# An encoder of two attention layers with experts: half of the output projection moved into the last attention steps, and layer 1's attention walked by key head in a fixed TensorE order

## The chip, the cores and the metric

The kernel runs on one core of a Trainium2 chip. The core's engines work from queues of their own, each in order: TensorE (PE; its weight loads are listed as PEld), VectorE (DVE), ScalarE (ACT), GpSimd (POOL) and SyncE (SP, which issues most DMAs). They wait for each other by semaphores. The metric is the time of one execution on the device in microseconds.

## The reference

Two layers over 512 tokens of width 1024, in float32, with 16 heads of 64. Each layer is a token mixer and a mixture of experts, both with a residual and a layer norm, scaled and shifted by a vector that comes from `c` (adaLN).

```python
for i in range(DEPTH):
    mod = c_act @ ada_w[i] + ada_b[i]
    sh1, sc1, g1, sh2, sc2, g2 = jnp.split(mod[:, None, :], 6, axis=-1)
    h = x * (1 + sc1) + sh1
    y = neighbourhood_mixer(...) if i == 0 else gqa_mixer(...)      # both end in  o @ w_o
    x = layer_norm(ALPHA * x + (1 + g1) * y, ln_g[i, 0], ln_b[i, 0])
    h = x * (1 + sc2) + sh2
    y = hierarchical_moe(h, ...)       # 4 groups of 8 experts: best group, best two experts
    x = layer_norm(ALPHA * x + (1 + g2) * y, ln_g[i, 1], ln_b[i, 1])
```

The neighbourhood mixer of layer 0 attends in a window of 8 rows by 16 columns with a bias. The mixer of layer 1 has 16 query heads over 4 key heads (4 queries share a key), with RMS-normed and rotated queries and keys, and attends to all 512 tokens.

## The kernel before

Tokens lie in four tiles `X[t]` of 128 rows. Most products are made in three terms of split operands, high and low halves (`hTH`/`hTL`, `wh`/`wl`, `oH`/`oL`): high by high, high by low, low by high. So one out-projection is 4 tiles x 2 column halves `h` x 8 blocks `k` x 3 terms = 192 matmuls of 512 columns, written to `pw` (`pj` in the changed kernel). ScalarE copies the high half, VectorE or GpSimd subtracts it for the low one.

**Layer 0.** `mixer0` first makes the values, then `neighbours` walks 32 steps n, head pair i = n // 4 and column block b = n % 4. `flow` writes TensorE's order, and with it VectorE's, by hand: the scores of step n + 1, then part of the filler, `turn(n)` (the transposes of the exponentials `pr`), adaLN work, more filler, and `weigh(n)` (the product with the values, in `po`). The filler is `STREAM`, the projections of the later heads, dealt out at `RATE` matmuls to a step. `close(i)` divides a head pair by its sum. The adaLN vectors `mod` are made of 24 column blocks j: `ADAV` lists those that VectorE makes by multiply-adds (`adav`), `ADAP` the pairs that TensorE makes (`adap`, one pair at the end of a step). `router_weights` folds the norm into the router's weights. Behind the steps come a `flush`, the two rows of `g1`, and then per tile t the out-projection `sums(t, h)`, the update of `X`, `turnX` (transposes of X), `logits`, and `router`, whose mask `Mb` VectorE makes in some 25 small operations and TensorE then sums. The order on TensorE is by hand there too.

**Experts.** Token rows are gathered by a matmul (`gc`), then the first and second expert matmuls (`gu`, `pd`) run. The 192 weight tiles of 1 MB of a layer come over SP's queue, in the order of a list (`W`): a transfer starts when the buffer that is next in that list comes free. Buffers are the five of `w0` and those of pools that are free in that phase: `wy` (`NWY` of them), `qs`, `wh`, `ot`. A pool that is opened where another was waits for the last reader of that other.

**Layer 1.** `mixer1` projects keys, values and the four query blocks, each of 4 query heads, in full before the attention; `attention(t)` then takes query tile t over all 16 heads. Within the layer the compiler's scheduler sets TensorE's order; no order is written by hand. The out-projection of tile t - 1 and its router are free to run beside the attention of tile t. `split_z` makes the gather's operands `zH` (ScalarE) and `zL` (GpSimd) as soon as a tile is normed.

## Time and profile before

| what | us |
|---|---|
| time, median of 3 runs | 1670.57 (1665.85 to 1672.82) |
| the profiled execution | 1673.29 |
| its span, first to last instruction | 1671.6 |
| TensorE, VectorE, ScalarE, GpSimd busy | 1574.7, 700.6, 437.6, 162.3 |
| mean granted clock of TensorE | 0.972 |
| layer 0: first out-projection matmul, first expert matmul | 296.06, 376.75 |
| layer 1: first record, first score, first expert matmul | 867.85, 981.59, 1164.38 |

A row of the timeline gives a start, a length, the engine, the line, the operation as out<-in, how many records it holds and, in brackets, the wait before it with the operation that ended it. Matmuls overlap, so the cost of one is the distance from its start to the next start, not its length. A matmul of plain float32 operands leaves two records. The granted clock is 1.00 at 2.4 GHz and 0.50 at 1.2 GHz; over a window it is a mean of the two.

### The profile page before, as it was taken

What the parts mean: (1) busy time and instruction counts of PE and PEld (TensorE: products, weight loads), DVE (VectorE), ACT (ScalarE), POOL (GpSimd) and SP (SyncE); (2) the same over time, 40 slices, a digit from 0 to 9 for tenths busy, and PEclk for the clock granted to TensorE, in tenths of its full rate; (3) what the DMA queues carried; (4) which work ended last, traced back from release to release, by engine and by line L of the source; (5) the groups of instructions that cost most, each with busy time, mean ns of one, the idle gap of its engine ahead of it and who ended that gap; (6) DMA issues with size and microseconds to landing.
All of it is one profiled execution on the core that took longest, in us unless ns stands there. A gap on an engine that the chain in (4) does not pass through costs nothing. (4 is left out here: it accounts for less than half of the span.)

```text
span 1671.6 us, 21362 instructions
## 1 busy us (share of the span) xinstructions
PE 1574.7 (94%) x8490; PEld 906.6 (54%) x8490; DVE 700.6 (42%) x1605; ACT 437.6 (26%) x934; POOL 162.3 (10%) x99
## 2 busy tenths in 40 slices
PE   7899997989999999999979989998999999999995
PEld 4676664773544545455448866766354545545442
DVE  3434545574232322323256865666432232323235
ACT  2343335231110111111134475453011111101112
POOL 2322212010000000000014250011000000000001
PEclk9999997999999999999989989999999999999997
DMA  9587872357999999999932000035899999999981
GB/s 328 196 309 269 331 306 104 137 202 295 417 419 420 419 419 420 419 419 420 420 125 102 26 1 25 1 125 206 368 416 420 420 420 420 419 420 420 419 332 51
DMA packets 76198, 493.17 MB, mean 295 GB/s; under 512 B 9876, under 2 KB 11284, under 8 KB 18876
## 3 DMA queue, kind: packets, MB, share of 16 engines
q1 hardware_dynamic: 71916, 485.05, 71.4%
q10 hardware_dynamic: 4176, 6.69, 1.2%
q8 instruction: 69, 1.13, 0.3%
q14 instruction: 37, 0.30, 0.1%
HBM read 489.61 MB, written 2.10 MB: 294 GB/s over the span
## 5 line engine op out<-in xcount | busy, mean ns | idle before, releaser
L300 PE MATMUL gu<-w,xT 128*64 128x512 f32 x2048 | 445.0, 592 | 0.0
L300 PEld LDWEIGHTS gu<-w,xT 128*64 128x64 f32 x2048 | 146.8, 137 | 291.6 <-issue 287.0
L300 PE MATMUL pd<-w,hx 128*64 128x512 f32 x1024 | 228.0, 598 | 0.0
L1391 DVE TENSOR_TENSOR h<-h,gu 128x512 f32<-128x512 f32 x32 | 22.0, 688 | 370.4 <-PE gu L300 370.4
L300 PEld LDWEIGHTS pd<-w,hx 128*64 128x64 f32 x1024 | 70.9, 137 | 140.3 <-issue 136.7
L300 PE MATMUL gc<-OH,zH 128*128 128x256 f32 x480 | 121.5, 291 | 2.6 <-DVE OH L1276 2.6
L300 PE MATMUL gc<-OH,zL 128*128 128x256 f32 x480 | 118.6, 284 | 0.0
L300 PE MATMUL gc<-YH,OT 128*128 128x512 f32 x244 | 104.2, 427 | 1.0 <-DVE X L1358 1.0
L1358 DVE TENSOR_TENSOR X<-X,gc 128x512 f32<-128x512 f32 x128 | 87.4, 688 | 39.3 <-PE gc L300 39.3
L300 PEld LDWEIGHTS gc<-OH,zH 128*128 128x128 f32 x480 | 92.5, 193 | 14.9 <-issue 11.4
L300 PE MATMUL gc<-YL,OT 128*128 128x512 f32 x244 | 96.3, 394 | 0.0
L300 PEld LDWEIGHTS gc<-OH,zL 128*128 128x128 f32 x480 | 92.6, 193 | 0.0
L300 PE MATMUL pw<-w,oH 128*128 128x512 f32 x256 | 86.3, 408 | 0.0
L1414 ACT ACTIVATE YH<-h 128x512 fp32r<-128x512 f32 x32 | 20.2, 630 | 233.6 <-DVE h L1413 233.6
L300 PE MATMUL pj<-wh,hTH 128*128 128x256 f32 (+1 forms) x272 | 71.2, 304 | 9.1 <-ACT hTH L419 4.0
L1294 ACT ACTIVATE xT<-gc,A 128x256 f32<-128x256 f32 x60 | 33.8, 566 | 173.9 <-PE gc L300 173.9
L300 PE MATMUL pj<-wl,hTH 128*128 128x256 f32 (+1 forms) x272 | 68.0, 292 | 0.0
L300 PE MATMUL pj<-wh,hTL 128*128 128x256 f32 (+1 forms) x272 | 65.6, 293 | 0.8 <-DVE hTL L427 0.8
L300 PEld LDWEIGHTS gc<-YH,OT 128*128 128x128 f32 x244 | 45.8, 188 | 37.3 <-DVE X L1358 15.8
L1292 DVE TENSOR_SCALAR xT<-gc,A 128x256 f32<-128x256 f32 x60 | 32.5, 545 | 76.9 <-ACT xT L1294 76.5
L1390 ACT ACTIVATE h<-gu 128x512 f32<-128x512 f32 x32 | 19.1, 597 | 173.0 <-PE gu L300 173.0
L303 PE MATMUL pt<-c_ident,pr 128*128 128x128 f32 x384 | 59.5, 283 | 2.1 <-ACT pr L862 2.0
(345 smaller groups left out, 2355.9 us busy)
## 6 DMA issues: line engine op xcount, KB each, us to landing
w<-in_gu SPq DMA_DIRECT2D x256, 1024.0 KB, 14.3
w<-in_dn SPq DMA_DIRECT2D x128, 1024.0 KB, 13.5
w<-in_ada SPq DMA_DIRECT2D x40, 1024.0 KB, 7.9
wq<-in_wqk SPq DMA_DIRECT2D x16, 512.0 KB, 3.6
w<-in_wo SPq DMA_DIRECT2D x8, 1024.0 KB, 5.8
w<-in_adaq SPq DMA_DIRECT2D x6, 1024.0 KB, 12.0
bias<-in_nab ACTq DMA_DIRECT2D x24, 256.0 KB, 3.4
w<-in_wq SPq DMA_DIRECT2D x4, 1024.0 KB, 4.9
```

Source lines behind the costliest of these rows:

```text
L300: return self.nc.tensor.matmul(out, l, r, start=start, stop=stop, **kw)
L303: self.nc.tensor.transpose(out, in_, self.ident)
L1292: nc.vector.tensor_scalar(xT[q][:, k, :], ps, s, b, op0=OP.mult, op1=OP.add)
L1294: nc.scalar.activation(xT[q][:, k, :], ps, AF.Identity, scale=s, bias=b)
L1358: nc.vector.tensor_tensor(X[t][:, c], X[t][:, c], ps, op=OP.add)
L1390: nc.scalar.activation(h, gu[0], AF.Silu)
L1391: nc.vector.tensor_tensor(h, h, gu[1], op=OP.mult)
L1414: nc.scalar.activation(YH[j][:, c], y, AF.Copy)
```

## The change

In layer 0 the weights of the output projection are split from step 26 on (`late`, `beside`). Steps 26 and 27 get no filler, and steps 28 to 31 get 24 matmuls each of the out-projection over the first half of its inputs, heads 0 to 7 (kh = 0), as filler. The second half (kh = 1) follows the attention, with logits and routers between. X is updated once for each half. Two more adaLN blocks go to VectorE, now three operations a step until step 23, and `router_weights` makes both of its sums on VectorE and in one matmul of 72 columns.

In layer 1 keys and values are projected together, query blocks 0 and 1 before the attention and 2 and 3 within it. The attention goes by key head c: 64 steps n = 16c + 4t + j, scores two steps ahead, TensorE in an order written by hand. Eight matmuls of a projection fill each of steps 3 to 14 of c = 0 and 1; five of the out-projection fill each step from 36 on, 140 of 192. X times the gain, plus the bias, is made beside it, on GpSimd for tiles 1 to 3. All four routers come behind the attention. `NWY` of layer 1 goes from one to three, `qs` from four to two, and in the weight list `wy` now stands first. The first gates are made before the first expert matmul instead of behind it.

```diff
-NWY = (3, 1)
+NWY = (3, 3)
...
-ADAV = [(0, 6), (0, 7), (0, 8), (0, 9), (1, 0), (1, 1), (1, 2)]
-ADAP = {4: [(0, 4), (0, 5)], 8: [(0, 10), (0, 11)], 12: [(1, 4), (1, 5)], 15: [(1, 6), (1, 7)], 19: [(1, 8), (1, 9)],
-        23: [(1, 10), (1, 11)], 26: [(1, 3)]}
...
+ADAP = {4: [(0, 4), (0, 5)], 8: [(0, 10), (0, 11)], 12: [(1, 5), (1, 6)], 15: [(1, 7), (1, 8)], 18: [(1, 9), (1, 10)], 21: [(1, 11)]}
...
-RATE = (18, 15)
+RATE = (18, 17, 24)
...
-            rate = RATE[n >= 12]
+            if n == 26:
+                need(STREAM[-1])
+                it = late()
+            rate = 0 if 26 <= n < 28 else RATE[(n >= 12) + (n >= 28)]
             fill(rate // 2)
             if b == 0 and i:
                 close(i - 1)
...
-                    adav(ADAV[i], b // 2, 2 * (b % 2) + k)
+            for k in range(3 * n, min(3 * n + 3, 8 * len(ADAV))):
+                adav(ADAV[k // 8], k % 8 // 4, k % 4)
             aside(n)
             fill(rate - rate // 2)
             if n in ADAP:
...
+        return it
...
         self.fold_cols(A2[:, 0], A2[:, 1], self.lnc[:, l, 0], self.lnc[:, l, 1], self.col[l][:, 2], self.col[l][:, 3])
-        ps = pp.tile([P, 36], F32, name="pt")
-        for k in range(KD):
-            self.mm(ps, bcast(A2[:, 1, k:k + 1], [P, P]), wr[:, k, :], k == 0, k == KD - 1)
-        nc.vector.tensor_tensor(rb, ps, self.rb[l], op=OP.add)
+        wb = pool.tile([P, S], F32, name=("dacc", "hf")[l], bufs=3 - l)[:, 0:KD * 36].rearrange("p (k n) -> p k n", k=KD)
+        sm = pool.tile([P, 2, 36], F32, name="wrs")
+        nc.vector.tensor_tensor(wb, wr, bcast(A2[:, 1, :, None], [P, KD, 36]), op=OP.mult)
         nc.vector.tensor_tensor(wr, wr, bcast(A2[:, 0, :, None], [P, KD, 36]), op=OP.mult)
-        ps = pp.tile([P, 36], F32, name="pt")
-        for k in range(KD):
-            self.mm(ps, bcast(self.Zo[:, 32:33], [P, P]), wr[:, k, :], k == 0, k == KD - 1)
-        nc.scalar.activation(cs, ps, AF.Copy)
+        for n, z in enumerate((wr, wb)):
+            nc.vector.tensor_reduce(sm[:, n, :], z.rearrange("p k n -> p n k"), axis=AX.X, op=OP.add)
+        ps = pp.tile([P, 2, 36], F32, name="pt")
+        self.mm(ps, bcast(self.Zo[:, 32:33], [P, P]), sm, True, True)
+        nc.vector.tensor_tensor(rb, ps[:, 1, :], self.rb[l], op=OP.add)
+        nc.scalar.activation(cs, ps[:, 0, :], AF.Copy)
 
     def fold_cols(self, out_s, out_b, g, b, sc, sh):
...
         def aside(n):
-            i, b = n // 4, n % 4
-            if b == 1 and i and i % 2 == 0:
-                self.accs, self.accl = [(j, accs.pop((l, j))) for l, j in ADAV[i - 2:i]], ADAV[i - 1][0]
+            while flushed[0] < len(ADAV) and 8 * min(flushed[0] + 2, len(ADAV)) <= 3 * n:
+                i = flushed[0]
+                self.accs, self.accl = [(j, accs.pop((l, j))) for l, j in ADAV[i:i + 2]], ADAV[i][0]
...
-            if n == 26:
-                self.router_weights(0, pp)
-            if n >= 28:
-                step()
-
-        self.flow(split, chunk, scores, turn, weigh, close, adav, adap, aside, done)
+            if n == 25:
+                self.router_weights(0, pp, pool)
+            beside(n)
+
+        flushed = [0]
+        it = self.flow(split, chunk, scores, turn, weigh, close, adav, adap, aside, late)
...
+        def project(c):
...
+                for k in range(KD):
+                    b = slice(256 * (k % 4), 256 * (k % 4) + 256)
...
+                    wh, wl = hl[c][1 + k // 4]
+                    for h, x in ((hH, wh), (hH, wl), (hL, wh)):
+                        self.mm(po, h[:, k, 128 * t:128 * t + 128], x[:, b], k == 0 and h is hH and x is wh, k == KD - 1 and h is hL)
+                        if h is hL and t == NT - 1 and k % 4 == 3 and c != 1:
+                            ahead(max(2, c + 1), k // 4)
+                        if k < KD - 1 or h is hH:
+                            yield
+                qq[c].append(rope(ps, t, 0, ss[c]))
+                yield
+
+        def keys(t):
...
+        def weigh(u):
+            c = u // 4
+            po[u] = pp.tile([P, 2, P], F32, name="po", bufs=1)
+            for kt in range(NT):
+                for y in range(2):
+                    self.mm(po[u][64 * y:64 * y + 64], V[:, kt, 64 * c:64 * c + 64], PT[u][:, kt, 2 * y:2 * y + 2, :],
+                            kt == 0, kt == 3)
...
+            queries(0, t)
+        scores(0)
+        scores(1)
+        for n in range(64):
+            c, i = n // 16, n % 16
+            if i == 0:
+                if c < 2:
+                    it = project(c + 2)
+                elif c == 2:
+                    hqs.close()
+                    step = late()
+                    it = halves()
+                else:
+                    self.free.append(nq)
+            if n == 24:
+                self.router_weights(1, pp, pool)
+            if 32 <= n < 36:
+                step(2)
+            elif 36 <= n < 44:
+                step(1)
+            k = (0 if i < 3 else 8) if c < 2 else 0 if n < 36 else 5
+            if n + 2 < 64:
+                scores(n + 2)
+            run(it, k - k // 2)
+            turn(n)
+            if c < 3 and 2 <= i < 6:
+                queries(c + 1, i - 2)
+                if c == 2 and i == 5:
+                    rps.close()
+            run(it, k // 2)
+            if n % 4 == 1 and n > 4:
+                finish(n // 4 - 1)
+        self.free.append(nq)
+        return it, lambda: finish(15)
 
     def scaled(self, pool, pp, dst, po, rz):
...
+                pw = pp.tile([P, F], F32, name="pj")
+                ks = range(KD) if kh is None else range(4 * kh, 4 * kh + 4)
+                for k in ks:
+                    oH, oL = (z[:, k % 2, :] for z in o[k // 2, t]) if l else (z[:, k % 4, :] for z in o[k // 4, t])
...
+                    for n, (a, b) in enumerate(((oH, wh), (oH, wl), (oL, wh))):
+                        self.mm(pw, a, b, k == ks[0] and n == 0, k == ks[-1] and n == 2)
+                        if k < ks[-1] or n < 2:
+                            yield
...
+                y = self.mod[0] if l else wk.tile([P, F], F32, name="y")
+                if l and kh == 0:
+                    eng = nc.gpsimd if t else nc.vector
+                    eng.tensor_tensor(x, x, gb[:, 0, c], op=OP.mult)
+                    eng.tensor_tensor(x, x, gb[:, 1, c], op=OP.add)
                 nc.vector.tensor_tensor(y, pw, g1[:, c], op=OP.mult)
-                nc.vector.scalar_tensor_tensor(x, x, ALPHA, y, op0=OP.mult, op1=OP.add)
+                if l or kh:
+                    nc.vector.tensor_tensor(x, x, y, op=OP.add)
+                else:
+                    nc.vector.scalar_tensor_tensor(x, x, ALPHA, y, op0=OP.mult, op1=OP.add)
+                yield
...
+            def halves():
+                for kh in range(2):
+                    for t in range(NT):
+                        for h in range(2):
+                            yield from sums(t, h, kh)
...
+            def late():
...
+                w, step = self.split_wo(l, whp)
+                lg, g1 = gain1()
+                if l:
+                    gb = wk.tile([P, 2, D], F32, name="gb")
+                    for n in range(2):
+                        for h in range(2):
+                            ps = pp.tile([P, F], F32, name="pj")
+                            self.row(ps, 0, 16 + 2 * n + h)
+                            nc.scalar.activation(gb[:, n, 512 * h:512 * h + 512], ps, AF.Copy, scale=ALPHA)
+                    return step
+                return halves()
...
+            def beside(n):
+                if n == 26 or n == 27:
+                    step(4)
+                    for t in range(2 * n - 52, 2 * n - 50):
+                        ready(0, t)
+                elif n > 27:
+                    step(2)
...
+                with tc.manual_schedule(engines={mybir.EngineType.PE}):
+                    it, finish = self.mixer1(st, qs, nq, pp, o, late, halves)
+                    hx = turnX(0)
+                    run(4)
+                    logits(0, lg[:, 0, :], hx)
+                    finish()
+                    for t in range(2, NT):
+                        run(6)
+                        hx = turnX(t - 1)
+                        run(8)
+                        logits(t - 1, lg[:, t - 1, :], hx)
+                        run(4)
+                        self.router(t - 2, wk, pp, "pt", lg[:, t - 2, :], rt)
+                        run(6)
+                    self.router(NT - 2, wk, pp, "pt", lg[:, NT - 2, :], rt)
+                    assert next(it, 0) == 0
+                st.close()
                 open_wy()
...
+            else:
+                rt = None
+                it = self.mixer0(oT, pp, late, beside)
+                open_wy()
                 with tc.manual_schedule(engines={mybir.EngineType.PE}):
...
+                        ready(1, t)
+                    self.free += [no] * 2
+                    for t in range(NT):
+                        run(6)
+                        hx = turnX(t - 1) if t else None
+                        run(8)
+                        if t:
+                            logits(t - 1, lg[:, t - 1, :], hx)
+                        run(4)
                         if t > 1:
                             self.router(t - 2, wk, pp, "pt", lg[:, t - 2, :], rt)
...
+                        run(6)
                     self.router(NT - 2, wk, pp, "pt", lg[:, NT - 2, :], rt)
-            else:
-                for t in range(NT):
-                    oTs.append([wk.tile([P, KD, P], F32R, name=n, bufs=2) for n in ("oH", "oL")])
-                    attention(t, at, pp, oTs[t])
-                    self.free.insert(0, nq)
-                    if t == 0:
-                        w, step = self.split_wo(l, wh)
-                        for _ in range(4):
-                            step()
-                    if t:
-                        project(t - 1, lg[:, t - 1, :], *oTs[t - 1])
-                        self.router(t - 1, wk, pp, "pt", lg[:, t - 1, :], rt)
-                st.close()
-                open_wy()
+                    assert next(it, 0) == 0
```

TensorE at the end of layer 0's attention: scores `ps`, transposes of `pr`, values product `po`; before, the last steps and the start of the out-projection.

```order
L303 MATMUL pt<-c_ident,pr 128x128 x4
L300 MATMUL po<-pts,V_94 64x128 x4
L303 MATMUL pt<-c_ident,pr 128x128 x4
L300 MATMUL po<-pts,V 64x128 x4
L303 MATMUL pt<-c_ident,rze 128x128 x4
L300 MATMUL pt<-dacc,Zo 32x512
L300 MATMUL pw<-mod_67,c_indc 128x512 x2
L300 MATMUL pw<-w_2314,oH 128x512
```

And changed, from the last scores into the filled steps.

```order
L302 MATMUL pt<-c_ident,pr 128x128 x4
L299 MATMUL po<-pts,V_97 64x128 x4
L299 MATMUL ps<-qk_2188,qk_2114 128x256 x2
L302 MATMUL pt<-c_ident,pr 128x128 x4
L299 MATMUL po<-pts,V 64x128 x4
L299 MATMUL ps<-qk_2188,qk_2114 128x256 x2
L299 MATMUL pj<-w_2277,oH 128x512
L299 MATMUL pj<-w_2077,oH 128x512
L299 MATMUL pj<-w_2277,oL 128x512
```

The out-projection stood behind the last `po` and the reciprocal's transposes (`rze`), and now its matmuls follow the scores within a step.

TensorE in layer 1's attention, a stretch before (scores `ps` in two terms, transposes of `pr`, out-projection `pw`).

```order
L300 MATMUL pw<-w_7314,oH 128x512
L300 MATMUL pw<-w_7923,oL 128x512
L300 MATMUL pw<-w_7923,oH 128x512
L300 MATMUL pw<-w_7314,oH 128x512
L303 MATMUL pt<-c_ident,pr 128x128 x4
L300 MATMUL ps<-kHH,w_6279 128x512
L303 MATMUL pt<-c_ident,pr 128x128 x4
L300 MATMUL ps<-kLL,w_6279 128x512
L303 MATMUL pt<-c_ident,pr 128x128 x4
```

And a stretch of the first key head, changed, with the query projection `pj`.

```order
L299 MATMUL pj<-wh,hTL 128x256
L299 MATMUL ps<-kHH,w_7005 128x512
L299 MATMUL ps<-kLL,w_7005 128x512
L299 MATMUL pj<-wh,hTH 128x256
L299 MATMUL pj<-wl,hTH 128x256
L299 MATMUL pj<-wh,hTL 128x256
L299 MATMUL pj<-wh,hTH 128x256
L302 MATMUL pt<-c_ident,pr 128x128 x4
```

Where kinds were mixed as they came free, a step now has a fixed pattern: two scores, part of the filler, four transposes, the rest of the filler.

TensorE at the end of layer 1's attention, before.

```order
L303 MATMUL pt<-c_ident,rze 128x128 x4
L300 MATMUL pw<-w_7932,oL 128x512
L300 MATMUL po<-PT,V 64x512 x7
L300 MATMUL pw<-w_7932,oH 128x512
L300 MATMUL pw<-w_7933,oH 128x512
L300 MATMUL pw<-w_7932,oL 128x512
```

And changed, with the first logits (`c_wr,hx`) ahead of the last values product.

```order
L299 MATMUL pj<-w_8405,oH 128x512
L299 MATMUL pj<-w_8404,oL 128x512
L299 MATMUL pt<-c_wr_80,hx 128x36 x8
L302 MATMUL pt<-c_ident,rze 128x128 x2
L299 MATMUL po<-PT,V 64x256 x8
L299 MATMUL pj<-w_8271,oH 128x512
L299 MATMUL pj<-w_8272,oH 128x512
L299 MATMUL pj<-w_8271,oL 128x512
```

Behind the last `po` stood 75 out-projection matmuls with the routers of tiles 2 and 3; now 52 stand there, and all four routers.

## Rows read from the trace of the kernel before

**Rows 1.** Windows: us, busy time (instructions) of the engines, granted clock, DMA share, GB/s.
```profile
core 0: us, PE busy (x) PEld busy (x) DVE busy (x) ACT busy (x) POOL busy (x), PEclk, DMA share, GB/s
...
270.00:296.00 26.00, 17.87 (x84) 9.62 (x82) 18.15 (x38) 13.52 (x33) 11.03 (x8) 0.67 0.35 137
...
868.00:906.00 38.00, 31.37 (x224) 29.71 (x225) 20.21 (x46) 20.85 (x33) 16.84 (x11) 0.85 0.28 94
...
982.00:1122.00 140.00, 137.81 (x713) 87.98 (x711) 88.14 (x198) 84.04 (x206) 27.89 (x23) 1.00 0.07 27
...
1165.00:1605.00 440.00, 436.81 (x2222) 208.97 (x2220) 135.35 (x266) 59.48 (x115) 0.00 (x0) 1.00 0.99 410
```

**Rows 2.** Timeline of TensorE: start and length in us, operation, [wait before it].
```profile
257.28 0.60 PE L303 MATMUL pt<-c_ident,pr 128*128 128x128 f32 x4
258.62 1.95 PE L300 MATMUL pt<-c_wr,A 128*128 128x36 f32 x16 [0.74 <-DVE A L408]
...
264.84 3.50 PE L300 MATMUL pt<-w,Z 128*32 128x512 f32 x16
...
277.45 1.12 PE L300 MATMUL po<-pts,V 128*64 128x128 f32 x8 [0.75 <-ACT pts L658]
...
281.91 1.12 PE L300 MATMUL po<-pts,V 128*64 128x128 f32 x8 [1.14 <-ACT pts L658]
...
288.36 1.00 PE L300 MATMUL po<-pts,V 128*64 128x128 f32 x8 [0.75 <-ACT pts L658]
...
293.20 3.04 PE L300 MATMUL pw<-mod,c_indc 128*128 128x512 f32 x4
...
296.87 0.63 PE L300 MATMUL pw<-w,oH 128*128 128x512 f32 x2
...
297.57 0.63 PE L300 MATMUL pw<-w,oH 128*128 128x512 f32 x2
```

**Rows 3.** Timeline of TensorE, layer 0's out-projection to the first expert matmul.
```profile
327.31 0.19 PE L300 MATMUL pt<-Mb,trib 128*128 128x32 bf16 x1 [3.11 <-DVE Mb L1126]
...
359.43 0.30 PE L303 MATMUL pt<-c_ident,X 128*128 128x128 f32 x1 [3.46 <-DVE Mb L1126]
...
376.75 1.51 PE L300 MATMUL gu<-w,xT 128*64 128x512 f32 x6
```

**Rows 4.** Timeline of TensorE, layer 1 from its first record to its first expert matmul.
```profile
867.85 1.94 PE L303 MATMUL pt<-c_ident,X 128*128 128x128 f32 x8 [6.23 <-ACTq L1169]
...
932.17 0.28 PE L300 MATMUL pj<-wl,hTH 128*128 128x256 f32 x1
932.29 0.28 PE L300 MATMUL pj<-wh,hTL 128*128 128x256 f32 x1
...
981.59 0.80 PE L300 MATMUL ps<-kHH,w 128*128 128x512 f32 x1
...
1118.65 3.65 PE L300 MATMUL po<-PT,V 128*64 128x512 f32 x14
...
1164.38 5.80 PE L300 MATMUL gu<-w,xT 128*64 128x512 f32 x26
```

**Rows 5.** Timelines of VectorE (DVE) and GpSimd (POOL), last router of layer 1.
```profile
1148.42 0.69 DVE L988 SCALAR_TENSOR_TENSOR X<-X,mod 128x512 f32<-128x512 f32 x1
...
1155.05 2.36 DVE L1109 SCALAR_TENSOR_TENSOR h<-h,c_iom 128x32 f32<-128x32 f32 x1
...
1157.94 0.19 DVE L1126 TENSOR_TENSOR Mb<-h 128x32 bf16<-128x32 f32 x1
...
1154.94 2.42 POOL L1067 TENSOR_TENSOR zL<-X,zH 128x1024 fp32r<-128x1024 f32 x1 [15.29 <-ACT zH L1066]
```

**Rows 6.** Groups by line and shape, 870 to 1122: busy us, mean ns, idle before.
```profile
L862 ACT ACTIVATE pr<-ps,st 128x512 f32<-128x512 f32 x64 | 43.7, 689 | 10.4 <-DVE st L860 9.3 <-ACT pr L862 0.7 <-PE pt L303 0.2
L869 ACT ACTIVATE PT<-pt 128x512 f32<-128x512 f32 x32 | 19.1, 598 | 16.7 <-PE pt L303 16.2
...
L860 DVE TENSOR_REDUCE st<-ps 128x1 f32<-128x512 f32 x64 | 42.4, 683 | 8.6 <-PE ps L300 8.3
```

More of the change, by code (lines that the diff above doesn't have):

```diff
@@ L584, in values, with neighbours @@
         return q0
-    def neighbours(self, pool, pp, hp, hH, hL, V, V6, oT, q0, done, step):
+    def neighbours(self, pool, pp, hp, hH, hL, V, V6, oT, q0, late, beside):
         nc, a = self.nc, self.a
@@ L880, in mixer1 @@
-        return attention
+        rps, hqs = ExitStack(), ExitStack()
+        pool, hq = rps.enter_context(left("rp1")), hqs.enter_context(left("hq1"))
+        rt = pool.tile([P, 4, NT, HD], F32, name="rt")
+        nc.sync.dma_start(rt[:, 0:2], a["rope"])
+        gn = pool.tile([P, 4, HD], F32, name="kk", bufs=8)
+        for i in range(4):
+            nc.sync.dma_start(gn[:, i, :], bcast(a["gain"][i:i + 1], [P, HD]))
+        hH = hq.tile([P, KD, S], F32R, name="hTH")
+        hL = hq.tile([P, KD, S], F32R, name="hTL")
@@ new lines, in finish, with run @@
+        def finish(u):
+            rest = close(u)
+            weigh(u)
+            rest()
+        def run(it, n):
+            for _ in range(n):
+                next(it, None)
+        for c in range(2):
+            for x in range(2):
+                ahead(c, x)
+        it = project(0)
+        run(it, 96)
+        it = project(1)
+        run(it, 8)
+        for t in range(NT):
+            keys(t)
+            run(it, 10)
+        for t in range(NT):
+            run(it, 12)
+            queries(0, t)
```

496 lines of the change are left out of this document (216 added, 280 removed).

## The prediction

> **What bounds the kernel now.** I read the windows first, since the average share of TensorE (94%) hides two stretches where it idles. In the mixture of experts TensorE is busy 436.81 of 440 us with DMA at 0.99 [rows 1]; nothing of the change lies there, and no gain can come from there. What the change can reach is the 376.75 us up to the first expert matmul of layer 0 [rows 3], and the 296.5 us from 867.85, the first TensorE record of layer 1, to 1164.38, its first expert matmul [rows 4].
>
> Then the timeline of TensorE shows where those stretches lose time. At the end of layer 0's attention the filler is used up: in the 26 us from 270 TensorE is busy 17.87 us, at a granted clock of 0.67, that is partly at 1.2 GHz [rows 1]. A step without filler lasts 4.46 us (277.45 to 281.91) [rows 2]: the exponentials, copies and waits set it, not the matmuls. Behind it the whole out-projection, 192 matmuls, runs from about 296 us with little beside it. It waits 3.11 and 3.46 us for the router's Mb from VectorE [rows 3].
>
> Layer 1 differs. Its projection part loses time: in the 38 us from 868 TensorE is busy 31.37, at a granted clock of 0.85 [rows 1]. From 982 to 1122 TensorE is busy 137.81 of 140 us, at full clock [rows 1]. There is no idle time in this attention into which work could go for nothing: what is moved there lengthens it.
>
> **Layer 0: removed.** One ADAP pair goes from TensorE to VectorE (3.50 us [rows 2]). The 16 more multiply-adds on VectorE I cost at nothing: projection matmuls run beside them. Without that cover they would be 16 x 0.69 us, by the operation of the same size in [rows 5], 11 us. The two chains of router_weights give way to one 72-column matmul: from 258.62 to 264.84 are 6.2 us [rows 2], of which I leave 0.3. The stream of projections then ends about one pair earlier, at 253.8 instead of 257.3 us, the first row of [rows 2].
>
> **Layer 0: moved.** Steps 26 and 27 have no filler and carry the splitting of wo and the rows of g1. I take the old unfilled step, 2 x 4.46 = 8.9, plus the 3.04 us of g1 [rows 2], which stood behind the attention before. In steps 28 to 31 each gets 24 out-projection matmuls. Three of them take 0.70 us (296.87 to 297.57) [rows 2], so 24 are 5.6 us. The step's own records (8 po, 4 score and 4 transpose records) add about 1.55 at full clock, an estimate from the 1.12 us that the po records alone take at half clock [rows 2], three such parts and little for switching. That is 7.15 us, longer than the 4.46 of the softmax chain, so TensorE sets the step: 28.6 for four. The chain from the last heads to oH of the second half (reciprocal, transposes, copy, multiply, split) is exposed: about 4 us, of the 4.84 from 288.36 to 293.20 before [rows 2], which hold a flush too. Sum: 253.8 + 0.3 + 8.9 + 3.0 + 28.6 + 4.0 = 298.6 us, where the second half starts. Before, the whole started at about 296.1 (296.87 less three matmuls).
>
> From there the old kernel needs 376.75 - 296.1 = 80.7 us to the first expert matmul. Without 96 matmuls (22.4 us) that is 58.3. Is this length still set by TensorE? VectorE has four times: two updates of X (4 operations of 0.69 [rows 5]), its statistics (1.6), logits (0.8), the router's some 25 small operations (4.6, at the 0.19 of the Mb operation there), and one of them held for 2.36 us while GpSimd writes zL [rows 5], 12 us in all. Four of those are 48 us, and 6.4 more lie between the last Mb and gu (1157.94 to 1164.38 in layer 1) [rows 4, 5]. That is 54.7, just under 58.3, so VectorE nearly sets it, and TensorE will wait at each router. I keep 58.3 and put 3 us on top for the sixteen pieces of wo that must be split by then, each a copy on ScalarE and a subtraction, and for stretches at half clock. First expert matmul: 298.6 + 58.3 + 3 = 359.9, a gain of **17 us**. Bounds: 22, if splits are hidden and the waits for Mb shrink; 5, if VectorE's 12 us per tile come on top of TensorE's 8 instead of beside them.
>
> **Layer 1: projections.** Before, 113.7 us pass from 867.85 to the first score at 981.59 [rows 4]. A 256-column matmul takes 0.12 us (932.17 to 932.29) [rows 4]. Moved into the attention: q2 and q3, 192 x 0.1175 = 22.6, their transposes 2.5, and the rows of g1, gain and bias, 7. Gone: the router chains, 5.2, and half the key transposes, 1.7. What is left on TensorE is 384 projection matmuls, 45 us, and transposes, 6. I add 19 for the start of the layer (5 us before the first projection), a start at half clock and the chain through the keys. So the first score comes after 70 us instead of 113.7.
>
> **Layer 1: attention.** It now holds 128 score matmuls (30 us), 140 instead of 117 out-projection matmuls (32.7), the 22.6 of q2 and q3, the value product (16 records of a half tile take 4.6 us, of which [rows 4] has 14 in 3.65, eight times: 36.6; split by key head it has as many columns), 344 transposes (31), the 7 us of rows, and about 13 for switching between kinds: 173. Full TensorE would end it at 70 + 173 = 243. But fixed order doesn't fill waits. Steps with no filler (0 to 2, 15 to 18, 31 to 35) run at the pace of ScalarE: exp 0.69, its accumulator, a copy 0.60 [rows 6], and other work, some 2 us a step. Step by step I get 12 unfilled steps at 2 to 3 us (29), 24 with projection filler at 2.8 (67), 28 with 5 out-projection matmuls at 3.0 (84): 180, so the end at 250 us. Before it ended at 1122.30 [rows 4], 254.5 us into the layer. VectorE and ScalarE come to some 130 us each in this stretch, by counting their operations at durations as in [rows 6].
>
> **Layer 1: tail.** Before, 42.1 us lie between that end and gu, with two routers already done. Now only 52 matmuls are left (12 us), but all four routers come behind the attention. VectorE's chain there: four routers with one held operation each (27), five X updates with statistics (10), logits and root (4), and 6.4 at the end, less 2 that run before the last value product: 45.5. So gu stands at 250 + 45.5 = 295.5 after the layer's start, against 296.5: **1 us gained**, taken as nothing. Bounds: 10 gained with fewer waits per step, 12 lost with 0.2 us more per step.
>
> The weight prefetch has a cost on the SP queue. Three tiles of the new wy pool now lead it, and they overlie the attention's own buffers, so the later ones in that in-order queue wait for its end. From there to gu are 45 us; a tile of 1 MB at the 410 GB/s of [rows 1] takes 2.6 us, so 17 fit, more than the 14 buffers. I charge nothing; if four tiles came late it would cost 10 us at the start of the experts.
>
> By the Trainium skill, page SBUF — State Buffer, section Who interferes with whom, a VectorE instruction with two SBUF inputs and a GpSimd instruction that reads SBUF exclude each other for the whole instruction. The held operation of [rows 5] agrees: 2.36 us beside a GpSimd record of 2.42. The change puts 12 updates of X (X times gain, plus bias) on GpSimd during the attention; at half of that 2.42 for half the size the rule could hold VectorE up to 14.5 us, and the sum would be up to that much worse where no slack covers it. I count none, since VectorE has a quarter of this stretch free.
>
> **Sum.** Against the profiled run of 1673.29 us (span 1671.6): 1673.3 - 17 - 0 = 1656.3. The median of the runs is 2.7 lower (1670.57), so I forecast **1654 us**.
>
> **Rivals.** *Layer 1 gains too*: if the fixed order runs as dense as the old one (97 to 98% busy), the attention takes 175 instead of 180, the start loses 5 less, and the tail overlaps its last routers: 12 us more, 1640. For it: layer 0's fixed order already runs dense with filler. Against it: the unfilled steps.
>
> *The gain is given back behind the attention*: VectorE sets both tails, as it nearly does by the sum above; layer 0 gains 8 and layer 1 loses 6: 1668. For it: both waits for Mb in [rows 3], with TensorE having twice the cover then.
>
> *Layer 1's fixed order stalls at the softmax*: transposes of step n are placed two steps behind its scores. Reduction and exponential alone take 0.68 + 0.69 [rows 6], and each waits in a queue that is three quarters full with rope, splits and copies. It decides from the point where that chain exceeds two steps (5.6 us): 0.5 us more per step is 64 x 0.5 = 32 us, at 1686. Against it: the lead of 5.6 is four times these two.
>
> That the change doesn't do what it says I exclude: the order of TensorE's instructions shows the filler.
>
> **How the numbers follow.** Forecast (1643 to 1662) 0.50; layer 1 gains too 0.14; given back 0.22; stall 0.14. A measurement of this kernel can tell some 0.5% (8.4 us) from no change: faster is the first two, 0.64; same 0.22; slower 0.14. The range reaches from 1637 (22 + 12 gained) to 1678 and leaves out most of the stall and a little at the bottom.
>
> **What would show it.** Right: gu of layer 0 near 360; 96 out-projection matmuls before the last po of layer 0; in layer 1 the first score about 70 us after its first record, the last value product at 250, and 45 us from there to gu; the expert stretches unchanged. Wrong: gu of layer 0 after 370 (VectorE set the tail), waits of pt for pr of over 0.3 us in most steps of layer 1, or expert matmuls waiting for weights at the start of layer 1.

## The result, and the profile after

The changed kernel takes 1690.09 us (median of three, 1688.24 to 1690.12) against 1670.57: a ratio of 1.0118, interval 1.0082 to 1.0154. It is slower by about 1.2% where 1% faster was forecast. The span of the profiled execution went from 1671.6 to 1688.3 us.

The windows of the changed kernel answer to [rows 1] (columns as there); the attention of layer 1 is cut in three.

```profile
core 0: us, PE busy (x) PEld busy (x) DVE busy (x) ACT busy (x) POOL busy (x), PEclk, DMA share, GB/s
270.00:296.00 26.00, 21.26 (x107) 13.95 (x106) 17.93 (x37) 14.00 (x35) 6.33 (x4) 0.92 0.04 11
938.00:1036.00 98.00, 87.93 (x598) 69.55 (x597) 67.70 (x154) 62.77 (x155) 20.88 (x17) 0.97 0.00 1
1036.00:1056.00 20.00, 4.92 (x20) 3.92 (x21) 14.73 (x20) 7.80 (x20) 17.64 (x14) 0.57 0.00 0
1056.00:1137.00 81.00, 81.00 (x485) 62.35 (x484) 51.07 (x102) 43.44 (x102) 5.12 (x7) 0.98 0.04 14
1183.00:1623.00 440.00, 436.11 (x2224) 209.12 (x2222) 133.74 (x264) 59.63 (x116) 0.00 (x0) 1.00 0.99 411
```

The last attention steps of layer 0 did get denser (21.26 us busy instead of 17.87, clock 0.92 instead of 0.67). The experts are unchanged. What is new is the third line: for 20 us in the middle of layer 1's attention TensorE does 4.9 us of work, while GpSimd is busy for 17.6 of them. The 81 us behind it have no gap at all.

TensorE's timeline of layer 0, in answer to [rows 2, 3]:

```profile
263.36 0.66 PE L302 MATMUL pt<-c_ident,pr 128*128 128x128 f32 x4
267.97 0.70 PE L299 MATMUL pt<-wrs,Zo 128*128 128x72 f32 x2 [3.95 <-DVE wrs L398]
...
270.81 3.68 PE L299 MATMUL pj<-mod,c_indc 128*128 128x512 f32 x4
...
279.71 0.73 PE L299 MATMUL pj<-w,oH 128*128 128x512 f32 x2
...
286.02 0.63 PE L302 MATMUL pt<-c_ident,rze 128*128 128x128 f32 x4 [3.25 <-DVE rze L970]
...
316.50 1.22 PE L299 MATMUL pj<-w,oH 128*128 128x512 f32 x2 [2.07 <-ACT oH L1104]
...
379.44 1.08 PE L299 MATMUL gu<-w,xT 128*64 128x512 f32 x4
```

The first expert matmul comes at 379.4, 2.7 us later than before instead of 17 earlier. Layer 1 still starts when it did (867.79, before 867.85), since layer 0's experts take 488.4 us from there instead of 491.1. Five traces of this document have the same program in layer 0 (this one and the four runs that change layer 1 alone), and their first expert matmul comes at 376.3 to 379.4, so a difference of up to 3 us in that place tells nothing. So layer 0 neither gained nor lost, and the 16.7 us of span come from layer 1, whose timeline answers to [rows 4]:

```profile
867.79 1.94 PE L302 MATMUL pt<-c_ident,X 128*128 128x128 f32 x8 [6.25 <-ACTq L1268]
...
938.41 0.48 PE L299 MATMUL ps<-kHH,w 128*128 128x512 f32 x1
...
947.88 1.09 PE L302 MATMUL pt<-c_ident,hf 128*128 128x128 f32 x4 [3.85 <-DVE hf L852]
...
1048.69 1.11 PE L302 MATMUL pt<-c_ident,hf 128*128 128x128 f32 x4 [11.28 <-DVE hf L852]
...
1134.97 1.95 PE L299 MATMUL po<-PT,V 128*64 128x256 f32 x16
...
1182.61 1.94 PE L299 MATMUL gu<-w,xT 128*64 128x512 f32 x8
```

The first score comes 70.6 us after the layer's first record, the last value product ends after 269.1 (before 254.5), and 45.7 us later the first expert matmul starts: 314.8 us in all, where it was 296.5. The experts behind it are 1.5 us shorter. All of the loss is in the attention, and 11.28 us of it is one wait, for the queries of the last key head.

VectorE in that hole:

```profile
1032.54 1.24 DVE L291 TENSOR_TENSOR rsu<-rsr 128x16 f32<-128x16 f32 x1
...
1037.95 1.26 DVE L295 TENSOR_TENSOR rsr<-rsr,rsu 128x16 f32<-128x16 f32 x1
1044.09 1.74 DVE L466 TENSOR_TENSOR w<-w,w 128x512 fp32r<-128x512 f32 x1 [4.88 <-POOL w L466]
1045.75 1.48 DVE L849 TENSOR_TENSOR kk<-kk,rsr 128x256 f32<-128x256 f32 x1
...
1048.09 0.55 DVE L852 TENSOR_TENSOR hf<-kk,hf 128x256 fp32r<-128x256 f32 x1
```

And GpSimd:

```profile
1032.03 2.95 POOL L1041 TENSOR_TENSOR X<-X,gb 128x512 f32<-128x512 f32 x2
1034.94 1.26 POOL L466 TENSOR_TENSOR w<-w,w 128x512 fp32r<-128x512 f32 x1
1036.16 1.80 POOL L1041 TENSOR_TENSOR X<-X,gb 128x512 f32<-128x512 f32 x1
1037.93 2.47 POOL L1042 TENSOR_TENSOR X<-X,gb 128x512 f32<-128x512 f32 x2
1040.36 1.25 POOL L466 TENSOR_TENSOR w<-w,w 128x512 fp32r<-128x512 f32 x1
1041.58 1.25 POOL L1042 TENSOR_TENSOR X<-X,gb 128x512 f32<-128x512 f32 x1
1042.80 1.25 POOL L466 TENSOR_TENSOR w<-w,w 128x512 fp32r<-128x512 f32 x1
```

Read from the bottom: GpSimd splits a piece of wo (L466), with updates of X (L1041, L1042) queued between the splits, and finishes at 1044.05; six updates, 8.5 us, stand in front of the last split. VectorE's own split waits 4.88 us for that (it writes into the slot that the piece leaves). Behind it in VectorE's queue stands `hf`, and for `hf` TensorE's written order has nothing to put in the meantime.

### The profile page after: what moved, and what is told of

It is laid out like the page before. It is cut to its first block, busy times and chain, and to the rows that moved or that the text cites. A ratio compares the mean times of both kernels' runs of the same rounds, so it can differ in the third digit from the quotient of the medians.

```text
span 1688.3 us, 21467 instructions
## 1 busy us (share of the span) xinstructions
PE 1559.0 (92%) x8514; PEld 912.9 (54%) x8514; DVE 741.5 (44%) x1646; ACT 445.5 (26%) x951; POOL 169.3 (10%) x107
## 5 line engine op out<-in xcount | busy, mean ns | idle before, releaser
L299 PE MATMUL pd<-w,hx 128*64 128x512 f32 x1024 | 227.4, 597 | 0.0
L299 PE MATMUL pj<-w,oH 128*128 128x512 f32 x256 | 89.1, 419 | 2.1 <-ACT oH L1104 2.1
L299 PE MATMUL pj<-wh,hTH 128*128 128x256 f32 (+1 forms) x208 | 53.7, 314 | 12.2 <-DVE t L781 3.5
L869 DVE TENSOR_REDUCE st<-ps 128x1 f32<-128x512 f32 x64 | 44.0, 689 | 34.6 <-PE ps L299 34.1
L1502 ACT ACTIVATE hx<-tp 128x512 f32<-128x512 f32 x32 | 19.0, 594 | 149.0 <-PE tp L302 128.8
```

The lines of the kernel that those rows point to most:

```text
L299: return self.nc.tensor.matmul(out, l, r, start=start, stop=stop, **kw)
L869: nc.vector.tensor_reduce(s[:, 0:1], ps, axis=AX.X, op=OP.max, negate=True)
L1502: nc.scalar.activation(hx, pt, AF.Copy)
```

## The experiments

The kernel before took 1669.4 to 1670.1 us beside these runs. Times are medians; the edits are on the changed kernel.

**The gain and bias of X on VectorE.**

```diff
-                    eng = nc.gpsimd if t else nc.vector
+                    eng = nc.vector
```

> In layer 1 the 12 operations X times gain, plus bias, of tiles 1 to 3 run on VectorE instead of GpSimd; nothing else differs from the changed kernel. Theory A (the 16 us from 1040 to 1056 in which TensorE is busy 4.26 us come from GpSimd, whose queue has these 12 operations of 1.25 to 1.5 us between the eight pieces of wo, and VectorE's own split waits 4.88 us for one of those pieces and holds up the softmax behind it): the hole shrinks by 10 us or more, 1676 to 1680 us in all, in spite of 8.3 us more on VectorE (12 x 0.69). Theory B (the fixed TensorE order is short of lead at every step, the hole is only where it shows): within 4 us of the changed kernel, 1686 to 1692.

1676.5 us, 1.0037 of before (1.0024 to 1.005): 13.6 of the lost us are back. The last value product ends 254.2 us after the layer's start, and the wait is less than half:

```profile
1037.20 1.11 PE L302 MATMUL pt<-c_ident,hf 128*128 128x128 f32 x4 [4.92 <-DVE hf L852]
```

**GpSimd's order in layer 1 written out as the program has it, splits first, with the same work on it.**

```diff
-                with tc.manual_schedule(engines={mybir.EngineType.PE}):
+                with tc.manual_schedule(engines={mybir.EngineType.PE, mybir.EngineType.Pool}):
```

> In layer 1 GpSimd too keeps the order of the program, so that the eight pieces of wo come before the 12 operations on X; the same operations on the same engines, only GpSimd's order differs. Theory A (order on GpSimd makes the hole at 1040 to 1056): 10 to 16 us faster than the changed kernel, 1674 to 1680. Theory B (short lead everywhere): within 4 us of it. Theory C (it is the amount of GpSimd work beside VectorE, each holding the other, not its order): 0 to 5 us faster, the hole spread over the following steps.

1679.3 us (1.0041; 1.0022 to 1.0059), 11 less. GpSimd still does every update of X, only not in front of the splits, and the wait for `hf` is 6.6 us. So most of the loss is where these operations stand, not the amount of work. The run alone doesn't tell the queue from VectorE and GpSimd holding each other, since the updates now run from 1064.2 us on, when these queries are done; the rows above do (see "The weighing of the rule" below).

**Layer 1's attention in the scheduler's order instead of the written one**, with the edit for VectorE and without it.

```diff
-                with tc.manual_schedule(engines={mybir.EngineType.PE}):
+                with ExitStack():
                     it, finish = self.mixer1(st, qs, nq, pp, o, late, halves)
```

With it:

> The gain and bias of X on VectorE, and layer 1's attention left to the scheduler's order on TensorE instead of the written one; layer 0 as in the changed kernel. To be held against the run with that edit alone (1676.5 us). Theory A: the written order costs nothing, since TensorE waits for nothing in most steps of it: 1675 to 1690 us. Theory B: the written order is itself a cost (the 3.9 us wait for the queries of the second head, the 4.9 us that were left of the hole): 1667 to 1673 us.

1664.3 us (0.9969; 0.9955 to 0.9983), 12.2 less than with that edit alone. The written order is a cost of its own. The same three stretches of the attention, cut before and behind the splitting of wo, in the written order:

```profile
935.00:1005.00 70.00, 61.45 (x442) 51.33 (x442) 47.97 (x119) 46.22 (x117) 8.40 (x7) 0.98 0.00 1
1005.00:1041.00 36.00, 29.43 (x175) 20.61 (x172) 28.31 (x57) 24.68 (x59) 14.49 (x11) 0.91 0.00 0
1041.00:1120.00 79.00, 78.93 (x483) 60.62 (x481) 56.16 (x109) 41.98 (x101) 5.14 (x7) 1.00 0.04 14
```

and in the scheduler's:

```profile
932.00:1002.00 70.00, 69.85 (x492) 55.99 (x493) 51.65 (x128) 50.01 (x129) 9.16 (x8) 1.00 0.00 1
1002.00:1038.00 36.00, 32.20 (x188) 21.92 (x186) 32.37 (x61) 27.15 (x66) 13.13 (x10) 1.00 0.00 0
1038.00:1107.00 69.00, 69.00 (x422) 53.31 (x422) 49.02 (x97) 35.43 (x87) 6.25 (x7) 1.00 0.05 16
```

TensorE idles 8.6 + 6.6 + 0.1 = 15.2 us in the first and 0.2 + 3.8 = 4.0 in the second; VectorE and ScalarE do the same work. With the written order TensorE waits 11.0 us in five places for the queries' `hf`; with the scheduler's 0.7. It has projection matmuls to put there, which the written order kept for later steps.

Without the edit for VectorE:

> The changed kernel with one thing undone: layer 1's attention left to the scheduler's order on TensorE. The gain and bias of X stay on GpSimd. Theory A: GpSimd's queue and the written order are two costs: the order is worth 12 us (1676.5 against 1664.3 with the gain on VectorE), the other 13.6 us stays: 1676 to 1680 us, with a hole of over 8 us on TensorE between 50 and 180 us after the layer's first record. Theory B: they are one cost seen twice, since what waits for GpSimd's queue only stops TensorE where the written order has nothing else to put there: 1662 to 1668 us, and no such hole. Theory C: without the edit on GpSimd the free order gives nothing: 1686 to 1692 us.

1679.1 us (1.0061; 1.0041 to 1.008), 11 less than the changed kernel. The hole behind GpSimd's queue is still there, with a wait of 9.6 us for `hf` and one of 4.7 us for `pr` ahead of it. So these are two costs, and they add up.

**Layer 0: the first half written behind the attention instead of into its steps.**

```diff
-            rate = 0 if 26 <= n < 28 else RATE[(n >= 12) + (n >= 28)]
+            rate = 0 if 26 <= n else RATE[(n >= 12) + (n >= 28)]
...
                     self.free += [no] * 2
+                    run(96)
```

> Layer 0 without the filler of steps 28 to 31: the same 96 matmuls run behind the attention instead, all else as in the changed kernel. Theory A (filled steps take 7.45 us where unfilled ones take 4.46, so the filler hides 22.4 - 4 x 3.0 = 10 us): 8 to 12 us slower than the changed kernel, 1698 to 1702. Theory B (VectorE sets what follows, and the updates of X hidden in the steps come out anyway): within 4 us of it.

1682.8 us (1.008; 1.0058 to 1.0102): 7.3 faster, where the expectations had slower or equal. The edit did something other than undo. The two stretches are written blocks of their own, and between blocks the scheduler chooses: it pulled 38 of the 96 matmuls forward into the gaps of the steps, from 273.8 on. The changed kernel from its first filler to its last value product, and from there to the first expert matmul:

```profile
279.00:312.00 33.00, 29.75 (x160) 22.32 (x160) 20.66 (x42) 10.78 (x28) 6.47 (x5) 1.00 0.04 8
312.00:379.00 67.00, 55.25 (x292) 46.02 (x288) 49.75 (x182) 22.66 (x51) 9.54 (x4) 0.82 0.54 220
```

and this one:

```profile
270.00:296.00 26.00, 23.01 (x140) 14.69 (x137) 21.07 (x45) 15.96 (x40) 8.86 (x6) 0.95 0.05 11
296.00:372.00 76.00, 68.19 (x352) 56.68 (x352) 56.77 (x190) 23.97 (x54) 9.54 (x4) 0.87 0.49 194
```

The last value product comes 16.3 us earlier (295.6 against 311.9), and the stretch behind it is only 8.3 longer (75.8 against 67.5). The 58 matmuls that moved into that stretch are 13.6 us at the 0.234 us of one. TensorE idled 11.8 us there and idles 7.8 now, and the granted clock rose from 0.82 to 0.87: the moved matmuls fill some of that.

**Layer 0: why the steps start late.** First the router's weights a whole step earlier (`n == 24` for `n == 25`):

> router_weights of layer 0 one step earlier, at step 24 instead of 25, where projections still fill. Theory A (the 3.95 us wait of TensorE for wrs at 267.97 is exposed because no filler is left behind it, and half clock follows it): 4 to 6 us faster than the changed kernel, 1684 to 1686. Theory B (ScalarE's copies of wo and of the heads set steps 25 to 27 anyway): within 2 us.

1688.2 us (1.0099; 1.0079 to 1.012). The matmul moved with VectorE's operations and waited 3.4 us there. Then VectorE's modulation work at the old pace:

```diff
-            for k in range(3 * n, min(3 * n + 3, 8 * len(ADAV))):
+            for k in range(pace(n), min(pace(n + 1), 8 * len(ADAV))):
...
+def pace(n):
+    return 2 * n if n < 16 else 32 + 4 * (n - 16)
```

> VectorE's modulation work of layer 0 at two operations a step up to step 15, as in the kernel before, and four a step from 16 to 25 instead of three a step throughout; all else as in the changed kernel. Theory A: the faster pace made the projection weights late in steps 4 to 12 (waits of 3 us such as that for the copied pts behind a late wq), and the stream of projections ends 3 to 4 us earlier with the old pace: last stream matmul at 257 to 259 instead of 261.8, 1685 to 1688 us. Theory B: the stream ends where it does because of what was moved ahead of its end, and four operations a step late are no better than three: last stream matmul at 260 to 264, 1688 to 1694 us.

1688.8 us (1.012; 1.0101 to 1.014). In this run the router's columns are read at step 13, before two of their blocks were added; the work is the same. The last matmul of the stream does start 5.4 us earlier, at 256.4, and the time doesn't move, since VectorE, now busy with the late blocks, gives the router's sums only 2 us earlier (265.9 for 267.9):

```profile
266.04 0.67 PE L303 MATMUL pt<-wrs,Zo 128*128 128x72 f32 x2 [7.45 <-DVE wrs L402]
```

Then both, VectorE's part two steps ahead of its matmul:

> Layer 0 only, else the changed kernel: VectorE's modulation work at two operations a step up to step 15 and four from 16 on (each pair flushed in the step that completes it, the router's columns taken at step 16), and VectorE's part of the router's weights at step 23 instead of 25, two steps ahead of its matmul. Theory A: in the changed kernel two things end side by side at step 25, the stream (last matmul at 261.8) and the wait for the router's weights (4.0 us at 268), and either edit alone left the time to the other one (1688.8 and 1688.2 us); both together put the first matmul of the output projection 7 to 9 us earlier, near 272, the last po near 305, the first expert matmul near 373: 1682 to 1685 us. Theory B: the stretch behind takes it back: 1686 to 1690 us.

1690.1 us (1.0119; 1.0099 to 1.014). The sums are there, but now the flush of the last block waits:

```profile
266.58 1.89 PE L303 MATMUL pt<-dacc,Zo 128*32 128x512 f32 x2 [4.59 <-DVE dacc L699]
```

Last, only VectorE's seven operations earlier, at the pace of the changed kernel; `rest` holds the matmul and what follows it, and stays at step 25:

```diff
-                self.router_weights(0, pp, pool)
+                rest[0]()
...
+            if n == 23:
+                rest.append(self.router_weights(0, pp, pool))
```

> The changed kernel with one thing moved: VectorE's seven operations for the router's weights of layer 0 stand at step 23 instead of 25, while the matmul that uses them stays at step 25; the modulation pace and TensorE's order are untouched. Theory A: the 4.0 us that TensorE waits for the summed weights at 268 is a loss of its own, hidden in the run that moved both by the wait moving along, and in the run with the old pace by VectorE's later modulation work: the first matmul of the output projection comes 3.5 to 5 us earlier (275 to 276), the first expert matmul of layer 0 near 375, 1684.5 to 1687 us. Theory B: the steps behind are bound by what VectorE and ScalarE do for them, and the time does not move: 1688 to 1692 us.

1685.9 us (1.0099; 1.0075 to 1.0123), 4.2 less, the first of the four that moved it. TensorE's rows are the same as in the changed kernel, in the same order:

```profile
264.18 0.34 PE L299 MATMUL pt<-wrs,Zo 128*128 128x72 f32 x2
...
267.16 1.98 PE L299 MATMUL pj<-mod,c_indc 128*128 128x512 f32 x4
...
274.82 0.73 PE L299 MATMUL pj<-w,oH 128*128 128x512 f32 x2
```

The sums are ready at 257.6, the wait is gone, and the filler starts at 274.8 instead of 279.7. So the wait of 3.95 us was a loss of its own; the runs before it had put another wait of VectorE in its place.

**Edits together.** VectorE's gain and bias with the first half behind the attention:

> The gain and bias of X in layer 1 on VectorE, and in layer 0 the first half of the output projection written behind the last attention steps instead of into them (TensorE's order then leaves the scheduler to pull some of it forward again). Theory A: the two causes lie in different layers and add up: 13.6 us from the first and 7.3 us from the second, 1690.1 - 20.9 = 1669 us, range 1666 to 1672; the first expert matmul of layer 0 near 371, the last value product of layer 1 near 254 us after its first record. Theory B: a part of each gain is the granted clock, which the other takes back: 1673 to 1677 us.

1669.9 us (1.0005; 0.9994 to 1.0016), as the sum of both (1669.2). Then also the copies of the last tile's transposes ahead of the hi-parts of z:

```diff
-                for t in range(NT - 1):
-                    split_z(t)
+                with tc.manual_schedule(engines={mybir.EngineType.Activation}):
+                    hx = turnX(NT - 1)
+                    for t in range(NT - 1):
+                        split_z(t)
```

> As the run before it, and in both layers ScalarE copies the transposes of the last row tile's X ahead of the three hi-parts of z, so that GpSimd's three lo-parts (2.4 us each) start behind that copy. Theory A: behind layer 1's attention TensorE waits 5.1 us for that copy and 3.6 us for the mask, with the hi-parts on ScalarE and the lo-parts on GpSimd in the way: 3 to 5 us less in layer 1, 0 to 4 in layer 0, 1661 to 1666 us; the gather of layer 1 starts 27 to 29 us after its last value product instead of 31.3. Theory B: VectorE's router chain sets that stretch, and the lo-parts come out last instead: 1667 to 1671 us, the gather 30 to 32 us after the last value product.

1664.9 us (0.9979; 0.9964 to 0.9993): the time of theory A, but not at its place. Layer 1's gather starts 30.2 us after the last value product instead of 31.3, as theory B had it; from there to the first expert matmul of layer 0 it is 73.5 instead of 75.9. The remaining 1.5 us lie ahead of the edit, and are within what such traces differ by. In layer 1 the wait only changed its owner. Without the edit:

```profile
1135.32 1.11 PE L302 MATMUL pt<-c_ident,X 128*128 128x128 f32 x4 [5.14 <-ACT hx L1056]
1140.06 0.19 PE L299 MATMUL pt<-Mb,trib 128*128 128x32 bf16 x1 [3.63 <-DVE Mb L1226]
```

and with it:

```profile
1136.89 0.19 PE L299 MATMUL pt<-Mb,trib 128*128 128x32 bf16 x1 [5.38 <-DVE Mb L1228]
```

since VectorE's router operations meet the three lo-parts on GpSimd. VectorE, then GpSimd:

```profile
1131.93 2.39 DVE L1211 SCALAR_TENSOR_TENSOR r<-r,c_iom 128x32 f32<-128x32 f32 x1
```

```profile
1129.62 6.95 POOL L1166 TENSOR_TENSOR zL<-X,zH 128x1024 fp32r<-128x1024 f32 x3 [19.12 <-issue]
```

All four, that is with the scheduler's order in layer 1 too:

> Four edits at once on the changed kernel: the gain and bias of X on VectorE, layer 1's attention in the scheduler's order, in layer 0 the first half of the output projection written behind the last steps, and the copies of the last tile's transposes ahead of the hi-parts in both layers. Theory A: additive, since each acts in its own stretch: 1664.3 - 7.3 - 4.9 = 1652 us, range 1650 to 1656. Theory B: the scheduler's order already takes part of the tail's gain: 1656 to 1660 us.

1652.3 us (0.9895; 0.9877 to 0.9914), as the sum has it. With the pace and the early sums added:

> The four edits of the run with the free order and all four, and the two of layer 0's front. Theory A: additive, 1652 less 5 to 7: 1645 to 1648 us. Theory B: the steps of layer 0 and the stretch behind them take the front's gain back, as with the pace alone: 1650 to 1655 us.

1653.6 us (0.9905; 0.9887 to 0.9923): the two together give nothing here either. With VectorE's sums at step 23 alone instead:

> The four edits of the fastest run so far (1652.3 us) and, in layer 0, VectorE's part of the router's weights at step 23 instead of 25. Theory A: the wait of 4 us goes here too: 1648 to 1650 us. Theory B: as with the two edits to layer 0's front together, no gain: 1651 to 1655 us.

**1647.1 us** (0.9869; 0.9848 to 0.9889), the fastest, 1.3% below the kernel before. Its first expert matmul stands at 363.0 in layer 0 (before 376.8), and in layer 1 at 286.2 us after the layer's first record (before 296.5). That is 13.8 us in layer 0, of the 17 forecast, and 10.3 in layer 1, where nothing was forecast. But it is not the change alone, freed of what held it up: in layer 1 the fixed TensorE order, half of the title, is undone, in layer 0 the scheduler places the filler, and the two edits to the tail and to the router's sums are new.

## Why the prediction was wrong

**Layer 0, 17 us forecast, nothing got.** The second half was to start at 298.6 and started at 316.5. By the terms of the sum:

| term | forecast | measured |
|---|---|---|
| transposes behind the stream | 253.8 | 263.4 |
| router's weights | 0.3 | 4.6 (264.0 to 268.6, behind 0.6 of transposes) |
| steps 26, 27 and g1 | 11.9 | 11.1 |
| steps 28 to 31, chain to the second half | 32.6 | 36.8 (279.7 to 316.5) |
| from there to gu | 61.3 | 62.9 |

- The failed step is "the stream of projections then ends about one pair earlier". The row of 3.50 us in [rows 2] stands behind the stream, so taking it away can't move the stream's end; and its 16 records are one block, where a pair leaves 32. What the change puts ahead of the end was left out: one block goes, but two flushes come (1.05 us each), and the stream now ends in step 24, before in step 26. From 20 us to the last matmul of the stream TensorE's busy time is nearly the same (226.7 us, before 227.4), but it idles 15.1 us instead of 9.7. Most of the difference lies in two stretches, first before, then after:

```profile
60.00:100.00 40.00, 37.37 (x202) 27.29 (x206) 14.39 (x40) 18.41 (x42) 13.46 (x6) 1.00 0.79 301
180.00:220.00 40.00, 38.05 (x253) 24.87 (x246) 21.71 (x45) 14.84 (x36) 9.72 (x4) 0.96 0.75 287
```

```profile
60.00:100.00 40.00, 34.83 (x177) 25.18 (x176) 14.75 (x40) 16.80 (x39) 12.80 (x6) 0.96 0.78 296
180.00:220.00 40.00, 35.62 (x217) 20.79 (x213) 18.23 (x40) 12.65 (x29) 8.57 (x5) 0.96 0.90 357
```

  The faster modulation pace on VectorE, 16 operations that I had costed at nothing, has a part in it: with the old pace the last matmul of the stream starts at 256.4 us, in the nine traces whose program is the same up to there at 258.0 to 261.8. What makes up the rest stays open.
- "Of which I leave 0.3" for the router's weights: the matmul is short, but its seven operations on VectorE are not, and TensorE's order puts the matmul right behind them. The run with those operations two steps earlier measured what the wait costs: 4.2 us.
- Steps of 7.15 us were nearly right (7.46, 7.45 and 6.83 for the last three), and so was the chain to the second half (4.3 us for 4.0). The wait of 3.25 us for `rze` in the first step was not in the sum.
- The 58.3 + 3 came out right in length, but not in what fills it. (The 54.7 for VectorE also add up to 54.4.) I had VectorE set the stretch; TensorE idles only 8.1 of the 62.9 us. It is busy for 54.8 us with work that took 48.0 before (70.4 less 22.4), since much of it runs at half speed. In the windows below the clock is 0.82 and 0.75, in the same windows before 1.00 and 0.83:

```profile
340.00:360.00 20.00, 16.05 (x86) 12.94 (x86) 16.91 (x75) 8.65 (x20) 4.75 (x2) 0.82 0.52 208
360.00:380.00 20.00, 15.85 (x91) 13.74 (x93) 13.36 (x52) 6.48 (x16) 2.38 (x1) 0.75 0.01 4
```

  The run with the first half behind the attention shows what follows: 13.6 us of matmuls put into this stretch lengthen it by 8.3, so work moved out of it into steps that it fills is not a gain of its whole length. In the fastest run the scheduler divides it.

**Layer 1, nothing forecast, 18 us lost.** The start (70.6 us for 70), the tail (45.7 for 45.5) and the work in between (TensorE busy 173.9 us for 173) were right, the last partly by luck: the 36.6 us for the value product were lengths, from start to start it takes 30.0, and the transposes and scores were put too low by as much. The failed step is "fixed order doesn't fill waits ... 180": it leaves seven us for waits, where there were 25, 10 of them up to 1036 and 15 in the hole. I had taken the waits from the softmax chain and given none to the other things that VectorE must bring in time: the rotated queries, whose transposes the written order puts right behind the VectorE operations that make them. Of the waits 16.3 us, in three places, are for their `hf`.

**The weighing of the rule.** The updates of X on GpSimd were counted at none, against up to 14.5 us by holding. The edit that takes them from GpSimd gives 13.6 us back, so none was wrong. But with the same updates on GpSimd in another order 11 of the 13.6 are back too, and the rows of the hole show what it consists of. Six updates, 8.5 us, stand in GpSimd's queue in front of the last split, for which VectorE waits. From there to `hf` VectorE's operations are held by about 2.3 us: 1.74, 1.48 and 0.55 us for forms that take 0.65, 0.41 and 0.41 from 1053.6 on, when GpSimd's updates are over. So most of the loss is a queue: splits behind updates, VectorE's split behind those, `hf` behind that. The Trainium skill, SBUF — State Buffer, Who interferes with whom, has the holding. The trace agrees with the rule itself (last section). That its price, 14.5 us, came near the 13.6 is coincidence, as the rows show.

**The rivals.** "The fixed order stalls at the softmax" had the time (1686) and the engine, but not the place: between the first score and the last value product TensorE waits once for `pr`, 1.2 us. The written order does cost 11 to 12 us, nearly all of it through the queries. "The gain given back behind the attention" did not happen in layer 1, and in layer 0 only in so far as there was no gain to give. "Layer 1 gains too" became true in the fastest run, by taking the fixed order away. Of the signs named, gu of layer 0 after 370 came, though not for the reason given with it (the stretch behind the attention took 62.9 us for 61.3); late weights didn't.

What stays open: which of VectorE's operations at steps 24 and 25 would have to move to use the earlier end of the stream as well. None of the runs with the old pace gained from it.

## What to carry to other kernels

When an engine's order is written by hand, list for each of its operations the last thing that another engine must bring, and how many operations stand in front of that in *its* queue. A short matmul placed right behind seven small VectorE operations costs their whole chain. Before moving work out of a stretch to save its length, look how long that engine idles in the stretch, and at what clock it runs there; and give filler to the scheduler where the gaps are known only after a run. Work that has no hurry (here gain times X) does not belong in front of work that has, even on an engine that is idle for nine tenths of the span.

## What the runs showed of the hardware

Holding between VectorE and GpSimd falls on operations still smaller than the one in [rows 5]: the 16-column products at 1032.54 and 1037.95 take 1.24 and 1.26 us beside GpSimd's updates of 1.25 us and more, and at most 0.18 in the four places each where layer 1 runs them before. `tensor_reduce` and a copy out of the accumulators in the same stretch keep their lengths, 0.68 and 0.67 us. By the Trainium skill, SBUF — State Buffer, Who interferes with whom, VectorE operations with two inputs in SBUF can be held by GpSimd's reads, and reductions can't. The trace agrees.

A wait of 4 us for one small result costs more than itself. In the changed kernel the granted clock is 0.84 over these 8 us, half speed from 267.4 on, and the four g1 records then take 3.68 us:

```profile
262.00:270.00 8.00, 4.05 (x29) 2.71 (x30) 4.51 (x12) 5.94 (x15) 2.56 (x2) 0.84 0.00 0
```

With the sums two steps earlier it stays at 1.00, and the same records take 1.98:

```profile
262.00:270.00 8.00, 6.16 (x41) 3.40 (x39) 3.38 (x13) 7.17 (x20) 2.54 (x2) 1.00 0.01 2
```
